# A two-layer gated-attention kernel: one more pair of projections by block products, and another order at the head of the output projection

## The chip, the cores and the metric

The kernel runs on one core of a Trainium2 chip. The metric is the time of one execution on the device in microseconds (us). A kernel is timed in several runs and the median is given. One further execution is profiled; its trace gives when each instruction started, how long it took and what ended the idle time before it. Five engines have a queue each and work their queue strictly in order: the tensor engine (PE, with its weight loads as PEld), the vector engine (DVE), the scalar engine (ACT), GpSimd (POOL) and the sync engine (SP), which only issues DMA transfers here.

## The reference, cut to what matters

One batch of 256 tokens with 2048 features goes through two layers, first gated linear attention (GLA), then retention, each with a gate path and an output projection, and a last RMS norm. Everything is float32. The change lies in the GLA layer:

```python
proj = rms_norm(h) @ w_in                     # 2048 -> q 1024, k 1024, v 4096, gate 4096
log_a = log_sigmoid((h @ w_a1) @ w_a2 + b_a) / 16
# four heads; per chunk of 64 tokens, with cum = cumsum(log_a):
scores = einsum('bhtk,bhsk,bhtsk->bhts', q, k, exp(cum_t - cum_s))    # causal
o      = scores @ v  + (q * exp(cum)) @ state
state  = exp(last) * state + (k * exp(last - cum)).T @ v
o      = o * rsqrt(mean(o * o) + eps) * head_g
out    = h + (o * silu(gate)) @ w_out         # 4096 -> 2048
```

## The kernel before, in words

**Tiles.** The 256 tokens are two halves of 128 partitions. A weight group is 2048 rows by 512 columns, cut into eight sub-blocks of 256 rows (512 KB each). A sub-block is loaded into one of eight `raw` buffers, and split into a rounded part `hi` (ACT, line 298) and a rest `lo` (DVE, line 299). There are four `hi` and four `lo` buffers, so a split can start only when the tensor engine is done with the sub-block four places earlier. Each product of float32 precision is three matmuls: left high by `hi`, left high by `lo`, left low by `hi`. A plain group is 8 sub-blocks x 2 row blocks x 2 token halves x 3 = 96 matmuls of 128x512.

**GLA heads.** `gla_head(h)` runs for four heads. It projects q and k (`gqk`), then for two groups of 512 columns the values (`gv`) and the gates (`gg`). Beside these, tasks in a queue called `side` are taken forward one step after each sub-block: the decay (`gla_decay`) and the scores (`gla_scores`). The scores work through seven levels (`w0` to `w6`) and a last product `w_x`: DVE makes exponents, ACT their exponential, DVE the products with q and k, PE a small matmul into `lv`. DVE then masks (`m`) what lies in `lv`, the seven levels are added into `s` on POOL (line 830, 14 instructions for a head), ACT and DVE split the sum into the pair `sc`, and `o_part` multiplies `sc` with a group's values (`go`, 9 matmuls). `og_part` norms and gates the result, and PE transposes (`got_tp`) bring it into `ogt`, the left side of the output projection.

**Pairs by block products.** Groups 5 and 7 (the second groups of heads 2 and 3) take values and gates together in `values_and_gates`: seven products of a half-size block scheme (`P1`, `P2`, `P3`, `P5` to `P8`, two sub-blocks of 6 matmuls each) and eight plain sub-blocks (`v4` to `v7`, `g4` to `g7`, 12 matmuls each) do the work of two plain groups. The string `UNIT` gives their order. The scheme needs sums of blocks of the left side (`xsum`, made by `make_sums` in the `rs` buffer) and of the weights: some are made by DMA that adds into a `raw` buffer (POOL's queue), some by DVE. Such a pair uses four PSUM banks A, B, C and V1, and a plain group two. The output projection of the first two heads (`ga`) is made of two such pairs in `out_pair`, whose left sums (`osum`) come from `ogt`. The residual x lies in `rs` from the start.

**What sets the order.** A scheduler puts each engine's instructions in an order that is fixed when the program is built; on the chip each engine takes its own in that order. An instruction marked `keep` is put behind whatever its engine was given before it in the code. The gate's SiLU in `g_evac` (line 688) is marked so, and the code of the last step of the scores, the copy into `sc` on ACT (line 724), stands right ahead of it for head 1. Weight splits are emitted three sub-blocks ahead of their use (`LOOK`).

Of the kernel before, what the change touches and what calls it, by code (L numbers as in the profile page):

```python
# [15 lines left out]
ALU = mybir.AluOpType  # L16

P = 128
# [46 lines left out]
def _plan():  # L65


    loads, subs = [], []

    def load(gid, j):  # L70
        loads.append((gid, j))
        return len(loads) - 1

    def use(c, pre=None, post=()):
        subs.append((c, pre, post))

    def plain(gid, js=range(NSUB)):
        for j in js:
            use(load(gid, j))

    def pair(g, v, q=None, order=None):
        order = (order or UNIT).split()
        x = [load(g, 0), load(g, 1)] if order[0] == "P1" else []
        z = []
        later = max(("P3", "P6"), key=order.index)
        for n, tok in enumerate(order):
            kind, i = tok[0], tok[1:]
            if kind in "qvg":
                plain({"q": q, "v": v, "g": g}[kind], [int(i)])
            elif tok == "z":  # L90
                z += [load(v, 2), load(v, 3)]
            elif tok == "P2":
                plain(g, [2, 3])
            else:
                if tok == "P1" and not x:
                    x += [load(g, 0), load(g, 1)]
                for j in range(2):
                    post = []
                    if tok == later:
                        post.append((z[j], (v, j)))  # L100
                    if tok == "P1":
                        post.append((x[j], (v, j)))
                    if tok == "P6":
                        post.append((x[j], (g, 2 + j)))
                    use(z[j] if tok in ("P3", "P7") else x[j], z[j] if tok == "P6" else None, post)

    def out_cols_of(name, half, cut, joint):
        for c in (0, 2):
            cols = [(name, half, c + n) for n in range(2)]
            if joint[c // 2]:  # L110
                pair(cols[1], cols[0])
                continue
            late = [range(NSUB)] if c or not cut else [range(cut), range(cut, NSUB)]
            for js in late:
                for x in cols:
                    plain(x, js)

    for half in range(2):
        for h in (2 * half, 2 * half + 1):
            plain(("aqk", h))  # L120
            for g in (2 * h, 2 * h + 1):
                if g in JOINT["a"]:
                    pair(("ag", g), ("av", g))
                else:
# [24 lines left out]
    buf = []  # L149
    for c in range(len(loads)):  # L150
        b = min([*range(NRAW), *_spare(loads[c])], key=lambda n: free[n])
        buf.append(b)
        free[b] = last[c]
    return loads, subs, places, last, buf


UNIT = "P1 v4 z P3 v5 P5 v6 P6 P2 v7 P7 g4 g5 P8 g6 g7"
MIXED = "q0 q1 P1 q2 q3 q4 z P5 q5 P6 q6 q7 P2 P3 v4 v5 v6 P7 v7 g4 g5 P8 g6 g7"
WHOLE = " ".join(f"q{j}" for j in range(NSUB)) + " " + UNIT


def ret_order(h):
# [4 lines left out]
HEAD = 4  # L167
EARLY = 2
JOINT = {
    "a": (5, 7),  # L170
    ("ao", 0): (True, True),
    ("ao", 1): (False, True),
    ("ro", 0): (False, True),
# [5 lines left out]
def kernel(  # L179
# [145 lines left out]
    def drain_side():  # L325
        while side:
            advance()
# [111 lines left out]
    def sums_in_v(name):  # L439
        return lambda n: v_p.tile([P, 2, QK, 2, P], F32R, tag="v", name=f"{name}{n}")  # L440

    def make_sums(lhs, name, where):
        s = cur["s"] = [None] * 4
        room = where(name)
        tt = nc.vector.tensor_tensor
        y = [t4_p.tile([P, QK, SEQ], F32, tag="t4", name=f"{name}_y{i}") for i in range(2)]
        for i in range(2):
            part = lhs[:, i * QK : (i + 1) * QK].bitcast(F32)
            tt(y[i], part[:, :, 0, :], part[:, :, 1, :], ALU.add)
# [4 lines left out]
        tt(f5, y[0][:, :, two], y[1][:, :, two], ALU.subtract)  # L454
        tt(f6, f5, y[0][:, :, one_], ALU.subtract)
        yield
        tt(f3, f6, y[1][:, :, one_], ALU.add)
        tt(f7, y[0][:, :, one_], y[0][:, :, two], ALU.subtract)
        yield
        for i, x in ((0, f3), (1, f5), (2, f6), (3, f7)):  # L460
            if i % 2 == 0:
                two_ = room(i // 2)
                s[i], s[i + 1] = two_[:, 0], two_[:, 1]
            keep(nc.scalar.activation(s[i][:, :, 0, :], x, AF.Copy))
            keep(tt(s[i][:, :, 1, :], x, s[i][:, :, 0, :].bitcast(F32), ALU.subtract))
            if i % 2:
                yield
# [285 lines left out]
    def gla_scores(h, box):  # L753
# [70 lines left out]
        nc.vector.tensor_scalar(s32[:, 1, :], ps[1][:, 3, :], SCALE, None, ALU.mult)  # L824
        yield
        for li, B in enumerate(LEVELS):
            for z in range(2):
                side_of = lambda a, h: a.rearrange("p (n h i) -> p n h i", h=2, i=B)[:, :, h, :]
                dst = side_of(s32[:, 2 * z, :], 1 - z)
                nc.gpsimd.tensor_tensor(dst, dst, side_of(m[:, li, :], z), ALU.add)  # L830
            if li == 3:
                yield
        yield
# [3 lines left out]
    def gla_head(h):  # L837
        hw = {}
        if h > 1:
            side.appendleft(gla_decay(h, hw))  # L840
        banks = None
        if h > 0:
            banks = acc(2, f"gqk{h}_ps", (P, 2, SEQ))
# [62 lines left out]
            )  # L906

        def joint_turn(tok):
            if tok == "v4":
                o_part(0)  # L910
            elif tok == "g5":
                o_part(1)
            else:
                advance()

        for gi in range(2):
            g = 2 * h + gi
            if g in JOINT["a"]:
                v = v_p.tile([P, 2, 2, GW], F32R, tag="v", name=f"gv{g}")
                sg = sg_p.tile([P, 2, GW], F32, tag="sg", name=f"gsg{g}")  # L920
                o = o_p.tile([P, 2, GW], F32, tag="o", name=f"ge{g}")
                vs.append(v)
                sgs.append(sg)
                banks = [slots[n] for n in (1, 0, 2, 3)]
                slots.rotate(-2)
                values_and_gates(
                    xhl, UNIT, acc(4, f"ge{g}_ps", which=banks), lambda: v, lambda: sg, lambda: o, r, r2, joint_turn
                )
                continue

            def v_hook(j):
                if h > 0 and gi == 1 and j == 1:
                    o_part(0)
                if h == 1 and gi == 1 and j > 1:
                    if j == 2:
                        cur["making"] = make_sums(ogt, "osum", sums_in_v)
                    if j < 6:
                        next(cur["making"])

            def g_hook(j):  # L940
# [4 lines left out]
                if gi == 1 and h == 1 and j == 3:  # L945
                    next(cur["making"])

            if h == 0 and gi == 1:
                drain_side()
# [36 lines left out]
    def out_pair(c, first, name, final=False):  # L986
# [36 lines left out]
        g = c + 1  # L1023
        cur["pin"] = final
        product(A, plain(0, 0), stop=True)
        advance()
        direct(lhs, (C, V1), 4)
        join(g, 0, A)
        advance()
        product(C, summed(0))  # L1030
        advance()
        direct(lhs, (C, V1), 5)
        drain_side()
        product(P5, summed(1), stop=True)
        direct(lhs, (C, V1), 6)
        for t in range(2):
            join(c, t, P5)
        product(A, summed(2), stop=True)
        product(B, plain(4, 0))
# [414 lines left out]

    for h in range(2):
        gla_head(h)
    slots = deque((2, 3, 0, 1))
    out_half(True, False, "ga", joint=JOINT["ao", 0])
    slots = deque((2, 3, 0, 1))
# [129 lines left out]
```

## Time and profile before

| what | value |
|---|---|
| time, median of 3 runs | 1372.14 us (1371.32 to 1372.71) |
| the profiled execution | 1371.82 us, span 1370.1 us |
| PE busy | 1360.1 us, 6564 matmuls |
| DVE, ACT, POOL busy | 1098.9, 846.7, 137.2 us |
| head 1: q and k / first group / second group | 126.98 to 152.24 / to 201.15 / to 248.90 us |
| output projection of the first two heads | 248.9 to 330.6 us |

The span leaves 1.7 us around it in the profiled execution. A busy time counts matmuls from issue to the modelled end, and they overlap; the time that one takes from the next is read from the distance of their starts in the timeline. A timeline row is start, length, engine, line, operation, output<-input, and in brackets the idle time ahead of it with what ended it.

### The profile page before, as it was taken

The page shows a single profiled execution, that of the slowest core. Times are in us where ns is not written, and L with a number is a line of the kernel's source. Part 1 is how long each engine was busy: PE and PEld are TensorE (multiplying, and loading weights), DVE is VectorE, ACT ScalarE, POOL GpSimd, SP SyncE. Part 2 cuts the span into 40 slices and gives each one's busy share as a digit, 9 for nine tenths or more (in the row PEclk, how much of TensorE's full clock was granted, in tenths as well). Part 3 has the DMA queues.
Part 4 walks back from the last instruction along what each step waited for, and adds up shares of the span by engine and source line. Part 5 has one row for each costly group of instructions (what it writes and reads, how often), then busy time and mean ns, then how long its engine had stood idle before and what let it go on. Part 6 is the DMA issues. An engine that isn't in the chain of part 4 may idle for free.

```text
span 1370.1 us, 18374 instructions
## 1 busy us (share of the span) xinstructions
PE 1360.1 (99%) x6564; PEld 1142.3 (83%) x6564; DVE 1098.9 (80%) x1520; ACT 846.7 (62%) x1119; POOL 137.2 (10%) x194
## 2 busy tenths in 40 slices
PE   9999999999999999999999999999999999999997
PEld 7888888888888888888888888888888888888886
DVE  6686795987878886769887988897867898889796
ACT  6576656656567756656666566655546666666565
POOL 1003020110021021001011010100101101010010
PEclk9999999999999999999999999999999999999999
DMA  9755565789658667868897878796798797879773
GB/s 363 255 175 168 169 208 184 154 251 316 202 154 259 201 207 180 326 169 232 260 336 199 259 203 249 209 320 212 172 365 219 245 253 208 268 188 322 237 177 124
DMA packets 84508, 315.04 MB, mean 230 GB/s; under 512 B 9776, under 2 KB 10800, under 8 KB 83136
## 3 DMA queue, kind: packets, MB, share of 16 engines
q1 hardware_dynamic: 67200, 241.63, 50.6%
q0 software_dynamic: 15920, 64.89, 23.7%
q10 hardware_dynamic: 1296, 7.35, 1.4%
q8 instruction: 51, 0.84, 0.2%
q14 instruction: 41, 0.34, 0.1%
HBM read 303.35 MB, written 10.49 MB: 229 GB/s over the span
## 4 chain that ended last, share of the span: by engine, by line
PE 99%; DMA 1%; DVE 0%; ACT 0%; issue 0%; DVEq 0%; ACTq 0%
PE rqk_ps L382 9%; PE re_ps L413 8%; PE re_ps L414 8%; PE re_ps L415 8%; PE rqk_ps L384 4%; PE gqk_ps L382 4%; PE gg_ps L342 3%; PE gv_ps L343 3%; PE gv_ps L341 3%; PE gv_ps L342 3%; PE gg_ps L343 3%; PE gg_ps L341 3%; PE gqk_ps L384 2%; PE ge_ps L415 2%; PE ge_ps L414 2%; PE ge_ps L413 2%
## 5 line engine op out<-in xcount | busy, mean ns | idle before, releaser
L299 DVE TENSOR_TENSOR lo<-raw,hi 128x1024 fp32r<-128x1024 f32 (+1 forms) x568 | 687.4, 1220 | 215.1 <-ACT hi L298 205.1
L298 ACT ACTIVATE hi<-raw 128x1024 fp32r<-128x1024 f32 (+1 forms) x568 | 596.3, 1056 | 398.9 <-PE rqk_ps L382 50.4
L382 PE MATMUL rqk_ps<-xhl,hi 128*128 128x512 f32 x512 | 160.0, 395 | 0.0
L415 PE MATMUL re_ps<-hi,xhl 128*128 128x512 f32 x352 | 137.1, 389 | 0.0
L414 PE MATMUL re_ps<-lo,xhl 128*128 128x512 f32 x352 | 137.1, 389 | 0.0
L413 PE MATMUL re_ps<-hi,xhl 128*128 128x512 f32 x352 | 132.3, 391 | 0.0
L310 POOL DMA_DIRECT2D raw<-in_w_all x90 | 78.0, 868 | 540.5 <-DVE lo L299 205.2
L384 PEld LDWEIGHTS rqk_ps<-xhl,lo 128*128 128x128 f32 x512 | 93.6, 188 | 20.3
L384 PE MATMUL rqk_ps<-xhl,lo 128*128 128x256 f32 x512 | 99.2, 279 | 0.0
L382 PEld LDWEIGHTS rqk_ps<-xhl,hi 128*128 128x128 f32 x512 | 80.7, 189 | 2.8
L382 PE MATMUL gqk_ps<-xhl,hi 128*128 128x512 f32 x256 | 79.5, 397 | 0.6 <-DVE xhl L550 0.6
L414 PEld LDWEIGHTS re_ps<-lo,xhl 128*128 128x128 f32 x352 | 66.1, 188 | 13.6
L415 PEld LDWEIGHTS re_ps<-hi,xhl 128*128 128x128 f32 x352 | 66.1, 188 | 13.6
L413 PEld LDWEIGHTS re_ps<-hi,xhl 128*128 128x128 f32 x352 | 65.9, 188 | 13.3
L342 PE MATMUL gg_ps<-lo,xhl 128*128 128x512 f32 x192 | 75.4, 393 | 0.0
L343 PE MATMUL gg_ps<-hi,xhl 128*128 128x512 f32 x192 | 75.1, 391 | 0.0
L342 PE MATMUL gv_ps<-lo,xhl 128*128 128x512 f32 x192 | 75.1, 391 | 0.0
L341 PE MATMUL gv_ps<-hi,xhl 128*128 128x512 f32 x192 | 75.0, 393 | 0.0
L341 PE MATMUL gg_ps<-hi,xhl 128*128 128x512 f32 x192 | 74.9, 391 | 0.0
L343 PE MATMUL gv_ps<-hi,xhl 128*128 128x512 f32 x192 | 74.8, 391 | 0.0
L830 POOL TENSOR_TENSOR s<-s,m 128x64 f32<-128x64 f32 x56 | 36.5, 684 | 232.3 <-DVE m L821 222.5
L384 PEld LDWEIGHTS gqk_ps<-xhl,lo 128*128 128x128 f32 x256 | 46.1, 188 | 10.0
(422 smaller groups left out, 2591.9 us busy)
## 6 DMA issues: line engine op xcount, KB each, us to landing
raw<-in_w_all SPq DMA_DIRECT2D x449, 512.0 KB, 4.9
raw<-in_w_all POOLq DMA_DIRECT2D x90, 512.0 KB, 7.2
resid<-in_x_n SPq DMA_DIRECT2D x2, 1024.0 KB, 9.8
gg<-in_gn_g POOLq DMA_DIRECT2D x8, 256.0 KB, 4.4
resid_x<-resid ACTq DMA_DIRECT2D x1, 2048.0 KB, 8.5
gb<-in_gn_b POOLq DMA_DIRECT2D x8, 256.0 KB, 4.9
gb_resid<-resid_x POOLq DMA_DIRECT2D x1, 2048.0 KB, 11.0
resid_g<-gb_resid ACTq DMA_DIRECT2D x1, 2048.0 KB, 9.0
```

Source lines behind the costliest of these rows:

```text
L298: a = nc.scalar.activation(hi[:, sl], src[:, sl], AF.Copy)
L299: b = nc.vector.tensor_tensor(lo[:, sl], src[:, sl], hi[:, sl].bitcast(F32), ALU.subtract)
L310: nc.gpsimd.dma_start(raws[n], block(key), accum_op=ALU.add)
L341: pin(mm(ps, xh, hi[:, q, :], start=kt == 0, stop=False, **onto))
L342: pin(mm(ps, xh, lo[:, q, :], start=False, stop=False, **onto))
L343: pin(mm(ps, xl, hi[:, q, :], start=False, stop=kt == end - 1, **onto))
L382: x = mm(ps[c], part, rhs[:, kt, :, :], start=kt == 0, stop=kt == NKT - 1)
L384: x = mm(ps[c][:, 0, :], part, rhs[:, kt, 0, :], start=False, stop=False)
L413: pin(mm(ps, xh, hi[:, q, :], start=start, stop=False, **again))
L414: pin(mm(ps, xh, lo[:, q, :], start=False, stop=False, **again))
L415: pin(mm(ps, xl, hi[:, q, :], start=False, stop=stop, **again))
L830: nc.gpsimd.tensor_tensor(dst, dst, side_of(m[:, li, :], z), ALU.add)
```

## The change

Group 3, the second group of head 1, is now taken as a pair as well. Its order is the string `FIRST`, with the product of scores and values of the first group after `v6` and that of the second after `g4`. The left sums `xsum1` for it are made in the `rs` buffer in head 1's q and k stage, over the residual, which is therefore loaded again from `x_n` after `P7`. The sums `osum` for the output projection are made in five steps during the pair. In the first pair of the output projection the three products that need only head 0's part of `ogt` (A, C, B) come first, with the string `HEADS` for its weights. The adding of the score levels goes from POOL, 14 instructions a head, to DVE, 7 a head, for all four heads.

```diff
+FIRST = "P1 v4 z P3 v5 P5 v6 P6 P2 v7 P7 P8 g4 g5 g6 g7"
+HEADS = "P1 z P3 P2 v4 v5 P5 v6 P6 v7 P7 g4 g5 P8 g6 g7"
 JOINT = {
-    "a": (5, 7),
+    "a": (3, 5, 7),
...
-                pair(cols[1], cols[0])
+                pair(cols[1], cols[0], order=HEADS if (name, half, c) == ("ao", 0, 0) else None)
...
-                    pair(("ag", g), ("av", g))
+                    pair(("ag", g), ("av", g), order=FIRST if g == 3 else None)
...
         for li, B in enumerate(LEVELS):
-            for z in range(2):
-                side_of = lambda a, h: a.rearrange("p (n h i) -> p n h i", h=2, i=B)[:, :, h, :]
-                dst = side_of(s32[:, 2 * z, :], 1 - z)
-                nc.gpsimd.tensor_tensor(dst, dst, side_of(m[:, li, :], z), ALU.add)
+            n = P // (2 * B)
+            dst = at(s32, B, (2 * P - B, 2), (2 * B, n), (1, B))
+            tt(dst, dst, at(m, li * P, (B, 2), (2 * B, n), (1, B)), ALU.add)
...
         if h > 1:
             side.appendleft(gla_decay(h, hw))
+        elif h == 1:
+            side.append(make_sums(xhl, "xsum1", sums_in_rs))
...
         def joint_turn(tok):
-            if tok == "v4":
+            if tok == ("v6" if h == 1 else "v4"):
                 o_part(0)
-            elif tok == "g5":
+            elif tok == ("g4" if h == 1 else "g5"):
                 o_part(1)
             else:
-                advance()
+                advance(2 if h == 1 and tok in ("g5", "g6", "g7") else 1)
+            if h == 1:
+                if tok == "P6":
+                    cur["making"] = make_sums(ogt, "osum", sums_in_v, "s_next")
+                if tok in ("P6", "P2", "v7", "P8", "g6"):
+                    next(cur["making"])
+                if tok == "P7":
+                    get_resid("resid_x")
...
-                if h == 1 and gi == 1 and j > 1:
-                    if j == 2:
-                        cur["making"] = make_sums(ogt, "osum", sums_in_v)
-                    if j < 6:
-                        next(cur["making"])
...
         product(A, plain(0, 0), stop=True)
-        advance()
-        direct(lhs, (C, V1), 4)
-        join(g, 0, A)
-        advance()
-        product(C, summed(0))
-        advance()
-        direct(lhs, (C, V1), 5)
-        drain_side()
-        product(P5, summed(1), stop=True)
...
+        if name == "ga" and c == 0:
+            advance()
+            product(C, summed(0))
+            advance()
+            product(B, plain(4, 0))
+            drain_side()
+            join(g, 0, A)
+            direct(lhs, (C, V1), 4)
+            direct(lhs, (C, V1), 5)
+            product(P5, summed(1), stop=True)
...
+        else:
...
     for h in range(2):
         gla_head(h)
+        cur["resid_at"] = x_n
+    cur["s"] = cur["s_next"]
```

Three places show what the change makes of the order. The first is the tensor engine at the end of head 1's first gate group; `lv` are the score levels, `go` is scores times values, `gg` and `gv` are the plain groups, `ge` is a pair's bank. Before, ahead of the first `go`:

```order
L343 MATMUL gv_ps_1947<-hi_1901,xhl 128x512
L341 MATMUL gv_ps_1946<-hi_1925,xhl 128x512
L342 MATMUL gv_ps_1946<-lo_1926,xhl 128x512
L698 MATMUL go_ps_1984<-gv_1741,sc_1850 128x512
L699 MATMUL go_ps_1984<-gv_1741,sc_1850 128x512
```

Now, at the same `go`:

```order
L417 MATMUL ge_ps_1956<-hi_1910,xhl 128x512
L766 MATMUL lv_1_1631<-w_4_1745 128x128 x2
L766 MATMUL lv_1_1631<-w_5_1778 128x128 x2
L766 MATMUL lv_1_1631<-w_6_1804 128x128 x2
L766 MATMUL lv_1_1631<-w_x 128x128 x2
L700 MATMUL go_ps_2082<-gv_1753,sc_1862 128x512
L701 MATMUL go_ps_2082<-gv_1753,sc_1862 128x512
L700 MATMUL go_ps_2083<-gv_1753,sc_1862 128x512
L701 MATMUL go_ps_2083<-gv_1753,sc_1862 128x512
L415 MATMUL ge_ps_1958<-hi_1930,xhl 128x512
```

Before, 42 matmuls of 128x512 stood between the last `lv` product and the first `go`; now none does, and `v4` (the last row, into bank C) stands behind the `go`.

The second is the vector engine from the last product of the scores' chain on; `osum` are the left sums of the output projection, `m` the masked levels, `s` their sum. Now:

```order
L817 TENSOR_TENSOR w_x<-w_x,qk_1527 128x256
L823 TENSOR_TENSOR m_1863<-lv_0_1630,mask 128x512
L301 TENSOR_TENSOR lo_1971<-raw_1842,hi_1970 128x1024
L451 TENSOR_TENSOR osum_y_2128<-ogt 128x1024
L301 TENSOR_TENSOR lo_1982<-raw_1865,hi_1981 128x1024
L451 TENSOR_TENSOR osum_y_2129<-ogt 128x1024
L825 TENSOR_TENSOR m_1863<-lv_1_1631,mask 128x384
L826 TENSOR_SCALAR s_1_1633<-lv_1_1631 128x128
L456 TENSOR_TENSOR osum_f_2156<-osum_y_2128,osum_y_2129 128x512
L831 TENSOR_TENSOR s_1_1633<-s_1_1633,m_1863 128x2x64
L831 TENSOR_TENSOR s_1_1633<-s_1_1633,m_1863 128x2x32x2
L831 TENSOR_TENSOR s_1_1633<-s_1_1633,m_1863 128x2x16x4
```

Four more of line 831 follow. Up to `osum_f` the order of the chain is the old one (there the split stood ahead of the first `m`), and the seven adds are new on this engine.

The third is the scalar engine behind the same chain; `gsg` is the SiLU of the gates. Now:

```order
L815 ACTIVATE w_x<-w_x 128x512
L300 ACTIVATE hi_1970<-raw_1842 128x1024
L300 ACTIVATE hi_1981<-raw_1865 128x1024
L726 ACTIVATE sc_1862<-s_1_1633 128x384
L690 ACT_TABLE_LOAD
L690 ACTIVATE gsg_1950<-gg_ps_1758,rr 128x512
L690 ACTIVATE gsg_1950<-gg_ps_1759,rr 128x512
```

The copy into `sc` is still followed by the table load and the two SiLU, but what stands in the two banks that they read is now awaited by `v4`, where before the next group had two other banks.

More of the change, by code (lines that the diff above doesn't have):

```diff
@@ L440, in sums_in_v, with make_sums @@
         return lambda n: v_p.tile([P, 2, QK, 2, P], F32R, tag="v", name=f"{name}{n}")
-    def make_sums(lhs, name, where):
-        s = cur["s"] = [None] * 4
+    def make_sums(lhs, name, where, key="s"):
+        s = cur[key] = [None] * 4
         room = where(name)
@@ L926, in gla_head @@
                 values_and_gates(
-                    xhl, UNIT, acc(4, f"ge{g}_ps", which=banks), lambda: v, lambda: sg, lambda: o, r, r2, joint_turn
+                    xhl, FIRST if h == 1 else UNIT, acc(4, f"ge{g}_ps", which=banks), lambda: v, lambda: sg, lambda: o, r, r2, joint_turn
                 )
@@ L944, in g_hook @@
                     o_part(1)
-                if gi == 1 and h == 1 and j == 3:
-                    next(cur["making"])
             if h == 0 and gi == 1:
@@ L1025, in out_pair @@
         product(A, plain(0, 0), stop=True)
-        advance()
-        direct(lhs, (C, V1), 4)
-        join(g, 0, A)
-        advance()
-        product(C, summed(0))
-        advance()
-        direct(lhs, (C, V1), 5)
-        drain_side()
-        product(P5, summed(1), stop=True)
[L1035 to L1039, printed above, removed]
+        if name == "ga" and c == 0:
[8 more added lines that the diff above has]
+            product(P5, summed(1), stop=True)
+            direct(lhs, (C, V1), 6)
+            for t in range(2):
+                join(c, t, P5)
+            product(A, summed(2), stop=True)
+        else:
+            advance()
+            direct(lhs, (C, V1), 4)
+            join(g, 0, A)
+            advance()
+            product(C, summed(0))
+            advance()
+            direct(lhs, (C, V1), 5)
+            drain_side()
+            product(P5, summed(1), stop=True)
+            direct(lhs, (C, V1), 6)
+            for t in range(2):
+                join(c, t, P5)
+            product(A, summed(2), stop=True)
+            product(B, plain(4, 0))
         join(c, 0, A, ALU.subtract)
```

## The prediction

> **What bounds the kernel now.** I read the page's busy line and chain of waits first, then the stages around the change.
>
> ```profile
> span 1370.1 us, 18374 instructions
> PE 1360.1 (99%) x6564; PEld 1142.3 (83%) x6564; DVE 1098.9 (80%) x1520; ACT 846.7 (62%) x1119; POOL 137.2 (10%) x194
> ...
> PE 99%; DMA 1%; DVE 0%; ACT 0%; issue 0%; DVEq 0%; ACTq 0%
> ```
>
> The chain that ended last is matmul work throughout: one matmul less is a gain, and any wait of the tensor engine is a loss that nothing later gives back. The stages of head 1 (q and k, first group, second group) and the first pair of the projection, in a table by stretches (PE, PEld, DVE, ACT, POOL busy, granted clock, DMA):
>
> ```profile
> 126.98:152.24 25.26, 25.26 (x146) 22.03 (x145) 16.44 (x31) 16.04 (x26) 0.00 (x0) 1.00 0.52 164
> 152.24:201.15 48.91, 48.91 (x239) 41.17 (x238) 41.44 (x73) 28.77 (x40) 7.03 (x11) 1.00 0.63 199
> 201.15:248.90 47.75, 47.75 (x214) 39.51 (x212) 29.59 (x42) 28.77 (x39) 3.79 (x7) 1.00 0.60 168
> 248.90:290.00 41.10, 41.10 (x192) 34.11 (x190) 36.22 (x40) 27.08 (x33) 5.17 (x6) 1.00 0.85 242
> ```
>
> PE is busy in all of it. DVE has 85% and 88% in the second and last, so it is the engine that can make PE wait if it gets more to do there. The timeline of PE at the first product of scores and values:
>
> ```profile
> 196.36 0.60 PE L764 MATMUL lv<-w 128*128 128x128 f32 x4
> 196.72 0.48 PE L342 MATMUL gg_ps<-lo,xhl 128*128 128x512 f32 x1
> 197.04 0.60 PE L764 MATMUL lv<-w_x 128*128 128x128 f32 x4
> ...
> 201.15 0.39 PE L341 MATMUL gv_ps<-hi,xhl 128*128 128x512 f32 x1
> ...
> 207.04 0.39 PE L698 MATMUL go_ps<-gv,sc 128*128 128x512 f32 x1
> ```
>
> From 201.15 to 207.04 stand 26 matmuls of 128x512, so each takes 5.89 / 26 = 0.2265 us, not the 0.39 of its row. A small one takes 0.36 / 4 = 0.09. Between the last score product (197.04) and the first `go` (207.04) PE has 10 us of other work.
>
> **What is removed.** A plain pair of groups is 192 matmuls, seven products and eight sub-blocks are 7 x 12 + 8 x 12 = 180. Twelve less: 12 x 0.2265 = 2.7 us. No other matmul is added or dropped.
>
> **The wait for the scores.** In the new order PE has nothing between the last `lv` product and `go`, so PE waits out the chain on DVE and ACT. That chain runs before as well, hidden behind PE's 10 us; its rows on DVE, POOL and ACT:
>
> ```profile
> 188.14 0.28 DVE L798 TENSOR_TENSOR w<-ref,lc 128x128 f32<-128x128 f32 x1
> 188.35 0.29 DVE L799 TENSOR_TENSOR w<-lc 128x128 f32<-128x128 f32 x1
> ...
> 190.22 1.22 DVE L299 TENSOR_TENSOR lo<-raw,hi 128x1024 fp32r<-128x1024 f32 x1
> 191.36 0.42 DVE L802 TENSOR_TENSOR w<-w,qk 128x256 f32<-128x256 f32 x1
> 191.70 0.42 DVE L803 TENSOR_TENSOR w<-w,qk 128x256 f32<-128x256 f32 x1
> ...
> 192.37 0.42 DVE L815 TENSOR_TENSOR w_x<-w_x,qk 128x256 f32<-128x256 f32 x1
> ...
> 195.41 1.32 DVE L449 TENSOR_TENSOR osum_y<-ogt 128x1024 f32<-128x1024 f32 x1 [0.88 <-PE lv L764]
> 196.65 1.37 DVE L299 TENSOR_TENSOR lo<-raw,hi 128x1024 fp32r<-128x1024 f32 x1
> 197.94 1.34 DVE L449 TENSOR_TENSOR osum_y<-ogt 128x1024 f32<-128x1024 f32 x1
> 199.21 0.54 DVE L823 TENSOR_TENSOR m<-lv,mask 128x384 f32<-128x384 f32 x1
> 199.67 0.28 DVE L824 TENSOR_SCALAR s<-lv 128x128 f32<-128x128 f32 x1
> 199.87 0.70 DVE L454 TENSOR_TENSOR osum_f<-osum_y,osum_y 128x512 f32<-128x512 f32 x1
> ```
> ```profile
> 194.68 8.45 POOL L830 TENSOR_TENSOR s<-s,m 128x64 f32<-128x64 f32 x14 [32.34 <-DVE m L821]
> ```
> ```profile
> 201.35 1.06 ACT L298 ACTIVATE hi<-raw 128x1024 fp32r<-128x1024 f32 x1 [1.63 <-PE gg_ps L343]
> 203.17 0.53 ACT L724 ACTIVATE sc<-s 128x384 fp32r<-128x384 f32 x1 [0.75 <-POOL s L830]
> 203.71 1.28 ACT L688 ACT_TABLE_LOAD   x1
> 205.00 1.27 ACT L688 ACTIVATE gsg<-gg_ps,rr 128x512 f32<-128x512 f32 x2
> ```
>
> By distances of starts, from the end of the product `w_x`: the first `m`, 512 elements, 0.6 (as `osum_f`, of the same size); split 1.14 (190.22 to 191.36); `osum_y` 1.24; split 1.14; `osum_y` 1.27; second `m` 0.46; `s` 0.20; `osum_f` 0.6. That is 6.7 us. Seven adds of 128 elements, each waiting for the one before: 0.21 us if they overlap like line 798, 0.33 if a whole row of 0.29 and a start must pass; I take 0.29, 2.0 us. The copy into `sc`, 0.53, and 0.1 for signals. In all 9.3 us, in which PE does the pair of `lv` matmuls, 0.2. **First term: 9.1 us.** Its floor is 8.2 (adds at 0.21 and no signals), its ceiling 10.6: from `w_x`'s end at 192.8 to the end of `sc` at 203.7 the old chain took 10.9, with POOL and an idle 0.88 and 0.75 in it.
>
> Ahead of it, `w_x` itself is late. In the new order the `w4` work can start only when the `lv` matmuls of `w0` have run, in the middle of the last gate sub-block, for its buffer is theirs; and the split of `v4`, ahead of it on DVE, ends some 0.9 us later still (a buffer free 6 matmuls earlier, then 1.06 on ACT, 1.14 on DVE). Then DVE has 13 rows of 128x256 at 0.34 (191.36 to 191.70), one `w_x` pair among them, two of 0.2 and a split: 0.9 + 4.8 + 0.4 + 1.1 = 7.2. PE has 8 small matmuls, 6 and 12 large ones: 0.7 + 4.1 = 4.8, and 0.5 of `lv` while it waits. **Second term: 1.9 us**, floor 0 (before, `w_x` was ready at 192.8, 4.3 us ahead of PE), ceiling 3 (the `lv` products not overlapped, and a signal each).
>
> Behind it, `v4` needs bank C, which the SiLU of the gates still reads, and the SiLU is queued behind the copy into `sc` and a table load: 1.29 (203.71 to 205.00) and 0.64, less four `go` matmuls of 0.9. **Third term: 1.0 us**, floor 0.8, ceiling 1.7. The Trainium skill, page "ScalarE: Activation LUTs", section "What ACT_TABLE_LOAD costs", puts a switch of sets at 1.28 us for the load and 1.38 for a drain, 2.66 in all. The row here has 1.28 and the next starts 0.01 after it, so this trace shows no drain; by the page the third term would be an estimated 2.4 and the total 1.4 higher.
>
> **The clock after the wait.** PE never idles so long here; the nearest row is the program's start:
>
> ```profile
> 1.00 4.03 PE L522 MATMUL warm_ps<-warm 128*128 128x128 f32 x20 [1.00 <-POOL lnone L524]
> ```
>
> Twenty small matmuls take 4.0 us, 0.20 each, against 0.09 in the middle. If an idle 9 us brings that back, PE loses about half of 4 us, 2.0, of which 0.9 falls on the `go` matmuls and so into the SiLU's wait. **Fourth term: 0.8 us**, floor 0, ceiling 2. The Trainium skill, "TensorE: Matmul & The Clock Gate", Part 1, says the same in mechanism: half rate after an idle window of about 3.4 us, full rate after about 3.4 us of work. By it the term would be an estimated 1.7 less the covered part.
>
> **The head of the projection.** The first pair now opens with six sub-blocks of 6 matmuls, 1.36 us each, and DVE's order up to the transposes of group 3 holds, besides their splits, head 1's norm and gating. DVE's groups of that stretch before, busy and mean:
>
> ```profile
> L299 DVE TENSOR_TENSOR lo<-raw,hi 128x1024 fp32r<-128x1024 f32 x23 | 28.2, 1228 | 14.8 <-ACT hi L298 14.8
> L896 DVE SCALAR_TENSOR_TENSOR go<-go,hr,gsg 128x512 f32<-128x512 f32 x4 | 2.9, 750 | 0.5 <-ACT gsg L688 0.4
> L502 DVE SCALAR_TENSOR_TENSOR ogt<-got_tp,smalls,ogt 128x256 fp32r<-128x256 f32 x6 | 2.8, 476 | 0.0
> ...
> L293 DVE TENSOR_TENSOR raw<-raw,raw 128x1024 f32<-128x1024 f32 x2 | 2.4, 1216 | 0.0
> ...
> L497 DVE TENSOR_TENSOR hr_nw<-hr_nw 128x2 f32<-128x2 f32 x3 | 0.5, 159 | 0.1
> ```
>
> Eight splits at 1.14 = 9.1, four gatings at 0.7 = 2.8, three `ogt` at 0.4 = 1.2, two weight sums 2.3, 13 small ones at 0.2 = 2.6, the gate's sum 0.6: 18.6 us. PE has 58 large and 8 small matmuls there, 13.9. DVE starts some 0.7 early, so PE is short by 4.0 if DVE does not get further ahead. **Fifth term: 3.0 us**, nearer to 4 than to none; floor 0 (before, 88% of DVE left no wait here), ceiling 5.
>
> **What is hidden.** `xsum1` on DVE in the q and k stage: two rows of 1.33, four of 0.7, four splits of 0.69, 8.2 us, into a stage in which DVE is free for 25.26 - 16.44 = 8.8; if that fails, PE waits up to 2. Six more splits and two weight sums (9.1 us of DVE, 6.4 of ACT) lie in the pair, where DVE was 62% busy; the stall gives them time. The adds of heads 2 and 3 cost DVE 2 us a head and free POOL. Six more adding transfers join POOL's queue, and the residual comes again:
>
> ```profile
> raw<-in_w_all POOLq DMA_DIRECT2D x90, 512.0 KB, 7.2
> ...
> gb_resid<-resid_x POOLq DMA_DIRECT2D x1, 2048.0 KB, 11.0
> ```
>
> It is issued after `P7`; 60 matmuls of the pair and more than 58 of the projection, 26 us, pass before the first join needs it, against 11. Without that cover the joins, and the splits behind them on DVE, would be up to 11 late.
>
> **Sum.** -2.7 + 9.1 + 1.9 + 1.0 + 0.8 + 3.0 = +13.1. The profiled execution took 1371.8 (1370.1 of span, 1.7 around it), so 1384.9; the median is 0.3 above it: 1385.2. I forecast **1385 us**, slower by 0.9%, with a chance of 0.68. All floors give -2.7 + 8.2 + 0 + 0.8 = +6.3, 1378.5; all ceilings -2.7 + 10.6 + 3 + 1.7 + 2 + 5 = +19.6, 1391.7.
>
> **Rivals.**
> 1. *Only the scores' wait.* The projection's head is covered and the clock holds: -2.7 + 9.1 + 1.9 + 1.0 = +9.3, 1381.4. For it: this scheduler's orders left PE no wait before. Against: DVE's 18.6 us. Chance 0.18.
> 2. *The other side: the scores come in time.* DVE's adds replace 8.45 us of POOL, `sc` is ready before the product P1 ends, and PE waits nowhere: 1372.1 - 2.7 = 1369.4, faster. It decides from the point where the last add ends before PE's last `lv` matmul plus 0.6. For it: before, DVE was 4.3 us ahead at `w_x`. Against: `m` reads what that very matmul writes, so at least 0.46 + 0.2 + 7 x 0.21 + 0.53 = 2.7 of chain always follow, and the split and `osum` rows stand in between. Chance 0.08, half of it below 1369.4.
> 3. *A second late transfer.* The residual's 2 MB or an adding transfer comes late on POOL's queue: up to 11 more, about 1392 to 1396. Against: 26 us of cover. Chance 0.06.
>
> **Chances and range.** What a measurement of this kernel can tell from no change is about 0.2%, 2.7 us. Faster 0.04 (half of rival 2), same 0.04, slower 0.92. The range from 1378.5 to 1391.5 holds the forecast and rival 1 with their unknown costs and leaves out rivals 2 and 3.
>
> **What would show it.** A PE row of `go` with an idle of about 9 us, released by ACT's copy into `sc` (term one); idle of about 2 us ahead of the `lv` products (two) and 1 us ahead of the first `v4` matmul (three); matmuls of 128x512 at 0.4 instead of 0.23 behind it (four); idle up to 2 us ahead of the `got_tp` transposes or the products in the projection's head (five); 6552 matmuls, and the rest as before. If `go` starts within 1 us of the last `lv` product, the prediction is wrong at its root.

## The result, and the profile after

The changed kernel takes 1387.5 us (median of 5 runs, 1386.34 to 1388.13) against 1372.14: 1.0109 times the time before, 95% interval 1.0097 to 1.0122. Forecast were 1385 us and 1378.5 to 1391.5. Its profiled execution has a span of 1385.7 us, 15.6 more than before. The page's busy line and its chain of waits:

```profile
span 1385.7 us, 18370 instructions
PE 1362.5 (98%) x6552; PEld 1142.0 (82%) x6552; DVE 1121.0 (81%) x1571; ACT 855.5 (62%) x1133; POOL 106.3 (8%) x145
...
PE 92%; DVE 3%; DMA 3%; ACT 1%; issue 1%; POOL 0%; DVEq 0%; ACTq 0%; POOLq 0%
```

The chain was 99% PE; now other engines hold 7% of it. The view of PE's waits (line, engine waited for; us in all, times, longest) names the places:

```profile
PE go_ps L700 <- ACT sc L726: 8.4, 1, 8.4
PE got_tp L710 <- DVE ogt L504: 1.6, 1, 1.6
PE gae_ps L416 <- DVE lo L301: 1.2, 2, 0.8
...
PE gae_p L416 <- DVE lo L301: 0.9, 1, 0.9
PE go_ps L700 <- ACT gv L1412: 0.6, 1, 0.6
```

The timeline of PE shows the long wait and what follows it:

```profile
203.87 0.71 PE L766 MATMUL lv<-w_x 128*128 128x128 f32 x4
212.99 0.80 PE L700 MATMUL go_ps<-gv,sc 128*128 128x512 f32 x1 [8.41 <-ACT sc L726]
213.59 0.63 PE L701 MATMUL go_ps<-gv,sc 128*128 128x512 f32 x1
...
214.99 0.80 PE L415 MATMUL ge_ps<-hi,xhl 128*128 128x512 f32 x1
215.59 0.63 PE L416 MATMUL ge_ps<-lo,xhl 128*128 128x512 f32 x1
216.01 0.63 PE L417 MATMUL ge_ps<-hi,xhl 128*128 128x512 f32 x1
```

From 213.59 on the starts lie 0.43 us apart, not 0.2265. The table by stretches has the reason in its clock column (the third number from the end), 0.50 from 206.71 to 216.95:

```profile
206.71:216.95 10.24, 3.96 (x9) 2.74 (x10) 7.83 (x16) 3.56 (x5) 0.00 (x0) 0.50 0.17 54
216.95:220.36 3.41, 3.41 (x17) 2.80 (x16) 0.27 (x1) 1.06 (x1) 0.00 (x0) 1.00 0.00 0
```

The chain on DVE and ACT during the wait:

```profile
203.72 0.70 DVE L823 TENSOR_TENSOR m<-lv,mask 128x512 f32<-128x512 f32 x1
204.32 1.23 DVE L301 TENSOR_TENSOR lo<-raw,hi 128x1024 fp32r<-128x1024 f32 x1
205.45 1.23 DVE L451 TENSOR_TENSOR osum_y<-ogt 128x1024 f32<-128x1024 f32 x1
...
209.52 0.70 DVE L456 TENSOR_TENSOR osum_f<-osum_y,osum_y 128x512 f32<-128x512 f32 x1
210.12 2.26 DVE L831 TENSOR_TENSOR s<-s,m 128x128 f32<-128x128 f32 x7
```
```profile
212.41 0.52 ACT L726 ACTIVATE sc<-s 128x384 fp32r<-128x384 f32 x1 [9.02 <-DVE s L831]
212.96 1.28 ACT L690 ACT_TABLE_LOAD   x1
214.25 1.26 ACT L690 ACTIVATE gsg<-gg_ps,rr 128x512 f32<-128x512 f32 x2
```

These are the forecast's rows, each without a gap; the first SiLU ends at about 214.9 and `v4` starts at 214.99.

Where the 15.6 us lie: the projection's first matmul starts at 258.95 instead of 248.89 (+10.1), the first matmul of head 2's q and k at 346.09 instead of 330.58 (+15.5), and from there to the end nothing is added. In matmul starts beyond their usual distance: 8.6 at `go`, 0.9 in the `lv` products, 2.1 in the 9 matmuls from it on (0.13 of this is the wait of `v4`, the rest the half speed), 1.6 at the second `go` (at 241 us), 3.8 at 268 to 277 us, 1.1 at 289 us and 0.45 more than before at the end of the second pair: 18.5, less 2.7 for the twelve matmuls, 15.8.

### The profile page after: what moved, and what is told of

The parts are those of the page before. It is cut to its first block, busy times and chain, and to the rows that moved or that the text cites. A ratio compares the mean times of both kernels' runs of the same rounds, so it can differ in the third digit from the quotient of the medians.

```text
span 1385.7 us, 18370 instructions
## 1 busy us (share of the span) xinstructions
PE 1362.5 (98%) x6552; PEld 1142.0 (82%) x6552; DVE 1121.0 (81%) x1571; ACT 855.5 (62%) x1133; POOL 106.3 (8%) x145
## 4 chain that ended last, share of the span: by engine, by line
PE 92%; DVE 3%; DMA 3%; ACT 1%; issue 1%; POOL 0%; DVEq 0%; ACTq 0%; POOLq 0%
PE rqk_ps L384 9%; PE re_ps L415 8%; PE re_ps L416 8%; PE re_ps L417 8%; PE rqk_ps L386 4%; PE gqk_ps L384 4%; PE gv_ps L345 3%; PE gv_ps L343 3%; PE gv_ps L344 3%; PE gg_ps L344 3%; PE gg_ps L345 3%; PE gg_ps L343 3%; PE ge_ps L415 3%; PE ge_ps L416 2%; PE ge_ps L417 2%; PE gqk_ps L386 2%
## 5 line engine op out<-in xcount | busy, mean ns | idle before, releaser
L301 DVE TENSOR_TENSOR lo<-raw,hi 128x1024 fp32r<-128x1024 f32 (+1 forms) x574 | 694.4, 1220 | 218.5 <-ACT hi L300 206.7
L312 POOL DMA_DIRECT2D raw<-in_w_all x96 | 83.0, 866 | 656.1 <-DVE lo L301 415.2
L344 PE MATMUL gv_ps<-lo,xhl 128*128 128x512 f32 x160 | 62.9, 393 | 0.0
L344 PE MATMUL gg_ps<-lo,xhl 128*128 128x512 f32 x160 | 62.8, 393 | 0.0
L345 PE MATMUL gv_ps<-hi,xhl 128*128 128x512 f32 x160 | 62.5, 392 | 0.0
L345 PE MATMUL gg_ps<-hi,xhl 128*128 128x512 f32 x160 | 62.5, 390 | 0.0
L343 PE MATMUL gg_ps<-hi,xhl 128*128 128x512 f32 x160 | 62.4, 392 | 0.0
L343 PE MATMUL gv_ps<-hi,xhl 128*128 128x512 f32 x160 | 62.4, 394 | 0.0
L416 PE MATMUL ge_ps<-lo,xhl 128*128 128x512 f32 x132 | 51.7, 392 | 0.0
## 6 DMA issues: line engine op xcount, KB each, us to landing
resid<-in_x_n SPq DMA_DIRECT2D x2, 1024.0 KB, 11.9
gb_resid<-resid_x POOLq DMA_DIRECT2D x1, 2048.0 KB, 11.9
```

Of the source, the lines that this page charges most:

```text
L301: b = nc.vector.tensor_tensor(lo[:, sl], src[:, sl], hi[:, sl].bitcast(F32), ALU.subtract)
L312: nc.gpsimd.dma_start(raws[n], block(key), accum_op=ALU.add)
L343: pin(mm(ps, xh, hi[:, q, :], start=kt == 0, stop=False, **onto))
L344: pin(mm(ps, xh, lo[:, q, :], start=False, stop=False, **onto))
L345: pin(mm(ps, xl, hi[:, q, :], start=False, stop=kt == end - 1, **onto))
L416: pin(mm(ps, xh, lo[:, q, :], start=False, stop=False, **again))
```

## The experiments

Ratios are to the kernel before, run beside each.

**The adds alone (e4).** Of the kernel before, only this is changed (14 instructions a head on GpSimd, 7 on DVE):

```
...
-                nc.gpsimd.tensor_tensor(dst, dst, side_of(m[:, li, :], z), ALU.add)
...
+            tt(dst, dst, at(m, li * P, (B, 2), (2 * B, n), (1, B)), ALU.add)
```

> The edit: the kernel before, with only the adding of the score levels moved from GpSimd (14 instructions a head) to the vector engine (7 a head), all else as before. If the adds cost nothing by themselves (the tensor engine has 10 us of other work between the last lv product and go in that order): 1372.1 us within 1 us. If the vector engine's 2 us a head reach the tensor engine: up to 4 x 2 = 8 us more, about 1374 to 1380.

1372.15 us, ratio 1.0003 (0.9994 to 1.0013). The adds cost nothing where PE has other work.

**What holds PE at the long wait? First, `go` out of the way (e2).** `pin` is `keep` for head 1's first group:

```
-                mm(ps[t], ah, v[:, s, 0, :], start=n == 0, stop=False)
+                pin(mm(ps[t], ah, v[:, s, 0, :], start=n == 0, stop=False))
```

> The edit: the changed kernel, but the four products of scores and values of the first group are pinned behind v6 in the tensor engine's order, so go no longer stands ahead of v4. Theory A (bank C): v4 still starts only when the first SiLU is done, at about 214.9 us of the span as now; go's 9 matmuls are then work that is no longer done under that wait, 1 us later: 1387.5 to 1389 us, an idle of about 10 us ahead of the first v4 matmul, released by the scalar engine's SiLU. Theory B (go waits for the scores): the tensor engine goes on with v4 to v6 and the wait is hidden: about 1378 us.

1393.07 us, 1.0155 (1.0137 to 1.0173). PE's waits, and the stretch of low clock:

```profile
PE ge_ps L415 <- ACT gsg L690: 10.4, 1, 10.4
PE go_ps L700 <- ACT gv L1412: 2.3, 1, 2.3
```
```profile
207.25:220.90 13.65, 6.15 (x15) 4.81 (x16) 7.05 (x16) 4.13 (x6) 0.00 (x0) 0.50 0.10 38
```

With `go` gone from the place, PE still idles, now 10.4 us and for the SiLU. So it is not the product of scores and values alone that waits for the scores: `v4`, and with it all that stands behind it in PE's queue, does so too, since `v4` needs a bank of the gates, the SiLU frees it, and the SiLU is queued behind the copy into `sc`. It came out dearer than either theory said: in the profiled execution 15 matmuls ran at half speed, and the second `go` waited 2.3 us. That execution was the longest of four (1390.37 to 1395.61), so the two sizes may be at their upper end.

**Then the SiLU out of the queue (e1).**

```
         yield
+        if h == 1:
+            yield
         split_scores(s32.rearrange("p b n -> p (b n)"), sc)
```

> The edit: the changed kernel, but the copy of head 1's scores into sc is written one step later, so that the two SiLU of the first group's gates are no longer pinned behind it on the scalar engine. Theory A (the queue of the scalar engine holds bank C: the tensor engine has no work because v4 needs the bank that the SiLU reads): the idle 8.4 us ahead of go and the half-clock matmuls behind it (about 2 us over their full-clock time) go, and nothing of like size takes their place: 1387.5 - 8.6 - 2.0 = about 1377 us. Theory B (the scores' chain on the vector engine is too long for whatever stands in front of go): v4 and P3 cover at most 24 x 0.227 = 5.4 us of the wait, so 3 us and the slow clock remain: about 1382 us.

1394.85 us, 1.0167 (1.0152 to 1.0183), slower than the change itself, and neither forecast. The long wait is gone, as theory A had it, but other waits stand elsewhere (first row: in all, times, longest):

```profile
PE ge_ps L415 <- ACT hi L300: 6.1, 3, 4.7
PE got_tp L710 <- DVE go L901: 5.3, 2, 4.4
```

Back from the 4.7 us at 233 us: the split `hi` waits for a transfer (first row), the transfers bunch, and POOL's adding transfers had stood 22.8 us for a weight sum on DVE, which DVE reached only at 217 us:

```profile
232.43 1.06 ACT L300 ACTIVATE hi<-raw 128x1024 fp32r<-128x1024 f32 x1 [2.59 <-DMA raw<-in_w_all]
```
```profile
199.00:225.00 26.00, 22.35 (x100) 16.93 (x99) 20.88 (x31) 18.93 (x22) 3.40 (x4) 1.00 0.48 135
225.00:258.00 33.00, 28.06 (x115) 22.38 (x114) 24.34 (x31) 20.38 (x28) 2.33 (x4) 0.90 0.98 313
```
```profile
218.87 0.87 POOL L312 DMA_DIRECT2D raw<-in_w_all  x1 [22.84 <-DVE raw L295]
```

The DMA share (last number but one) goes from 0.48 to 0.98. DVE had hardly a gap from 208 to 231 us. That the long wait had given DVE time which the new order needs (theory D in what follows) is the reading; this run alone doesn't show it, for the edit did more than move the copy. The two SiLU now stand among the exponentials of the last score levels, so ACT loads its tables four times there, 1.28 us each (at 198.43, 200.44, 202.38 and 205.33 us), where the change has one load (212.96), and DVE stood 1.98 and 2.19 us for ACT before 206 us.

**The sums off DVE (e5).** The four sums `osum_f` likewise:

```
+        su = nc.gpsimd.tensor_tensor if key == "s_next" else tt
-            tt(y[i], part[:, :, 0, :], part[:, :, 1, :], ALU.add)
+            su(y[i], part[:, :, 0, :], part[:, :, 1, :], ALU.add)
```

> The edit: the changed kernel, but the sums osum of the output projection's left side (two of 128x1024, four of 128x512) are added on GpSimd instead of the vector engine; nothing else. Theory C (the rows of the vector engine that stand between the last lv product and sc set the length of the first wait): two rows of 1.14 us and one of 0.6 leave the chain, so the idle ahead of go falls from 8.4 to about 5.5 us and the time to about 1384.5 us; less still if the later waits shrink with it. Rival: the sums come too late from the slower GpSimd for the third product of the reordered head, and that wait takes the gain: 1387 to 1390 us.

1389.43 us, 1.0129 (1.0114 to 1.0144), and the wait at `go` grew to 9.6 us. The two splits in the chain and GpSimd's rows beside them:

```profile
204.34 6.05 DVE L301 TENSOR_TENSOR lo<-raw,hi 128x1024 fp32r<-128x1024 f32 x2
```
```profile
203.12 6.18 POOL L452 TENSOR_TENSOR osum_y<-ogt 128x1024 f32<-128x1024 f32 x2 [6.85 <-PE lv L767]
```

Two splits take 2.35 us elsewhere; beside a GpSimd sum they took 6.05. So this run did not shorten the chain and doesn't test theory C.

**The sums later on DVE (e9).** For the `osum` of the first pair alone:

```
-            tt(y[i], part[:, :, 0, :], part[:, :, 1, :], ALU.add)
+            (keep if key == "s_next" else lambda x: x)(tt(y[i], part[:, :, 0, :], part[:, :, 1, :], ALU.add))
```

> The edit: the changed kernel, but the two first sums osum_y of the output projection's left side are pinned on the vector engine where the code has them (behind the splits of P6's time), so that no row of osum stands between the last lv product and sc any more; they stay on the vector engine, GpSimd has nothing to do beside it. Theory C (the vector engine's rows between the last lv product and sc set the length of the first wait; the longer wait of the fifth experiment came from GpSimd slowing the vector engine's rows): the idle ahead of go falls by 1.14 + 1.14 + 0.6 = 2.9 us to 5.5, and the time to 1384.5 us. If C is wrong, the idle stays at 8.4 us or above, and the time at 1387 us or more.

```profile
PE go_ps L700 <- ACT sc L726: 5.7, 1, 5.7
PE got_tp L710 <- DVE go L899: 5.3, 2, 4.6
```
```profile
204.56 2.35 DVE L301 TENSOR_TENSOR lo<-raw,hi 128x1024 fp32r<-128x1024 f32 x2
```

The wait fell by 2.7 us, as theory C said: DVE's rows set its length. The time did not: 1393.21 us, 1.0149 (1.0132 to 1.0166). The projection starts 2.5 us earlier than in the change (256.44 against 258.95) but takes 7.5 us longer (to 351.04 against 346.09): the transposes in its head wait 5.3 us for the gating, for which they had not waited at all. Two things differ on DVE there. The sums now stand in its way at 234 to 253 us. And the steps of head 1's norm, which the gating needs, are placed differently: in the change three splits stand between them, and from the first step to the gating they take 5.9 us (258.81 to 264.76); here seven splits and two weight sums stand between them, and they take 11.9 us (261.97 to 273.88). How much of the loss comes from the sums and how much from that order is not shown.

**The idle filled (e8, e11).** Matmuls whose results nobody reads, behind the last `lv` product; 45 on top of e2 (e11), 90 on the changed kernel (e8):

```
         pair_mm(ps[1][:, 3, :], w)
+        if h == 1:
+            idle = mis_p.tile([P, P], F32, tag="mis", name="idle")
+            for _ in range(45):
+                mm(idle, w[:, 1, 0:P], w[:, 1, SEQ : SEQ + P], start=True, stop=True)
```

> The edit: the changed kernel with 90 matmuls of 128x128 into an unused bank put between head 1's last lv product and what follows (their results are not read; they take about 9 us of the 10 us for which v4 must wait). Clock theory (the half-speed matmuls behind the first wait come from the idle itself): the first v4 matmuls run at 0.227 us instead of 0.43 and the granted clock stays at 1.00 there; v4 still starts when the SiLU has freed its bank, at about 215 us, and go's 9 matmuls come later: against the second experiment (1393.1 us, go also behind v4, 14 matmuls at half speed) about 3 us less. If the slow matmuls had another cause (the weights' transfers, the bank), they stay at 0.43 us and the time at about 1393 us.

> The edit: the kernel of the second experiment (go pinned behind v6, 1393.1 us, idle of 10.4 us ahead of v4 and 14 matmuls of 0.43 us behind it) with 45 matmuls (90 instructions of about 0.11 us, 10 us; twice that many in the eighth were 20 us and outlasted the wait) into an unused bank right behind the last lv product. Clock theory: the idle is gone or under 1 us, v4 starts at about 215 us as before, its matmuls take 0.227 us and the granted clock stays 1.00: 2.8 us less than the second experiment, about 1390.3 us. Otherwise about 1393 us.

In e8 the 90 became 180 instructions of 20 us, which outlasted the wait: 1397.28 us, 1.0188 (1.0173 to 1.0204), no measure of the time, though the clock stayed at 1.00. e11, on top of e2:

```profile
204.32 10.21 PE L824 MATMUL idle<-w_x 128*128 128x128 f32 x90
214.41 0.50 PE L415 MATMUL ge_ps<-hi,xhl 128*128 128x512 f32 x1
214.75 0.39 PE L416 MATMUL ge_ps<-lo,xhl 128*128 128x512 f32 x1
214.98 0.40 PE L417 MATMUL ge_ps<-hi,xhl 128*128 128x512 f32 x1
```

1388.97 us, 1.0124 (1.0109 to 1.0139), 4.1 less than e2 with 90 instructions more; e2's runs lie so far apart that the size is rough. `v4` starts about where it did (214.41 against 214.75), and at full speed: the starts lie 0.23 us apart, not 0.43. The second `go` then waited no 2.3 us either. Idle costs twice: while it lasts, and in the slow matmuls behind it.

**The old head of the projection (e3).** With the old branch of `out_pair` to match:

```
-                pair(cols[1], cols[0], order=HEADS if (name, half, c) == ("ao", 0, 0) else None)
+                pair(cols[1], cols[0], order=None)
```

> The edit: the changed kernel with the old order of the first pair of the output projection (A, v4, C, v5, P5 and so on; table of weights to match). If the reordered head (six sub-blocks of 6 matmuls at the start against a vector engine with 18.6 us of work) is what makes the waits of 3.8 us at 268 to 277 us and of 1.1 us at 289 us, they go: about 1383 us, and with the first wait untouched 1386 at the least change. If it is the vector engine's work alone (norm, gating, sums of the left side, which come in either order), the waits stay or move to other rows: 1386.5 to 1388.5 us.

1389.16 us, 1.0129 (1.0112 to 1.0146), above both forecasts.

```profile
PE gae_ps L417 <- DVE ogt L504: 1.6, 1, 1.6
PE gae_ps L415 <- ACT gsg L1422: 1.2, 1, 1.2
PE got_tp L710 <- DVE go L899: 1.1, 2, 0.9
```

The waits of the head stay, in other rows: `HEADS` is not their cause. In either order DVE's and ACT's rows end them; that DVE's amount of work is the cause is argued from this, not shown.

**Scores earlier (e7, e10) and the DVE relieved (e6).** In e7 head 1's decay starts in its q and k stage, with `osum` on GpSimd; e10 has the decay and e9's later sums; e6 is e1 with `osum` on GpSimd.

```
-        if h > 1:
+        if h > 0:
             side.appendleft(gla_decay(h, hw))
...
```

> The edit: the kernel of the first experiment (SiLU ahead of the copy into sc, 1394.9 us) with the sums osum on GpSimd as well. Theory D (without the first wait the vector engine is busy from 208 to 231 us without a gap, frees the raw buffers late, and so the transfers and the tensor engine come late): some 4 us of vector work leave that stretch, the wait of 4.9 us at 233 us shrinks by about as much, 1389 to 1391 us. Rival E (the transfers themselves are the bound, 98% busy from 225 to 258 us there): no change beyond 1 us, 1394 to 1396 us.

> The edit: the changed kernel with head 1's decay started three steps earlier (in its q and k stage, as in heads 2 and 3), so that the scores' steps and sc are written three sub-blocks ahead of the SiLU; and the sums osum on GpSimd. If the first wait is all that the new order lacks: 1387.5 less 8.6, 2.0 and some of the later waits, 1374 to 1377 us, and go no longer waits. If the vector engine's total work in this part is the deeper bound (as theory D has it), the wait comes back elsewhere, as in the first experiment: 1383 to 1392 us.

> The edit: the decay of head 1 three steps earlier (as in the seventh experiment) and osum_y later (as in the ninth); nothing on GpSimd. In the seventh experiment the rows of the vector engine beside GpSimd took 2.3 to 3.0 us instead of 1.22, about 7 us in all, and the tensor engine waited 4.7 us for late transfers at 234 us. If it was this slowing that made the buffers and transfers late, the wait at 234 us goes, no first wait comes back, and the waits of the projection's head (4.4 us) remain: 1375 to 1379 us. If the vector engine's total work is too much even at full speed, as theory D says: 1380 to 1386 us.

e6: 1390.39 us, 1.0133 (1.0116 to 1.015), in theory D's range, and 4.5 less than e1. The wait for transfers, 4.7 us in e1, is 0.4 here, so the transfers were not a bound by themselves (rival E); but with GpSimd slowing DVE and new waits the run tells little more. e7: 1386.41 us, 1.0103 (1.0088 to 1.0118): `go` no longer stalls, and 4.5 us of late transfers come in its place. e10: 1381.73 us, 1.0072 (1.0057 to 1.0087), the best version, yet in theory D's range:

```profile
PE got_tp L710 <- DVE go L899: 5.2, 2, 4.6
PE gae_p L416 <- DVE lo L301: 1.4, 1, 1.4
...
PE gae_ps L416 <- DVE lo L301: 0.8, 1, 0.8
```

Group 3 takes 48.0 us there (199.29 to 247.26), with little waiting, and the projection starts 1.6 us earlier than in the kernel before (248.89). All of the loss lies in the projection, which takes 92.3 us (to 339.59) against 81.7. DVE's order in its head has the norm's small steps between splits:

```profile
251.96 0.15 DVE L891 TENSOR_TENSOR hm<-sso 128x2 f32<-128x2 f32 x1
...
257.13 0.15 DVE L499 TENSOR_TENSOR hr_nw<-hr_nw 128x2 f32<-128x2 f32 x1
257.20 1.22 DVE L301 TENSOR_TENSOR lo<-raw,hi 128x1024 fp32r<-128x1024 f32 x1
...
263.87 2.74 DVE L899 SCALAR_TENSOR_TENSOR go<-go,hr,gsg 128x512 f32<-128x512 f32 x4
```

The same steps in the change, with three splits between them where e10 has nine rows of 1.14 us:

```profile
258.81 0.15 DVE L891 TENSOR_TENSOR hm<-sso 128x2 f32<-128x2 f32 x1
...
264.76 2.74 DVE L899 SCALAR_TENSOR_TENSOR go<-go,hr,gsg 128x512 f32<-128x512 f32 x4
```

So e10 doesn't show that DVE has too much work in all (theory D): the order of this chain is a rival. With the change's order the gating would come 6.0 us earlier (11.9 less 5.9, an estimate from these rows), more than the 5.2 us of wait; what the rows put off by it would then hold up is not known, and e10 with that order was not run.

**The norm's steps on GpSimd (e12).** On top of e10, for head 1's `rsqrt`:

```
...
+            g = nc.gpsimd
+            for it in range(3):
+                g.tensor_tensor(a, b, b, ALU.mult)
+                g.tensor_tensor(a, a, m, ALU.mult)
+                g.tensor_scalar(a, a, -0.5, 1.5, ALU.mult, ALU.add)
+                g.tensor_tensor(y if it == 2 else b, a, b, ALU.mult)
...
```

> The edit: the kernel of the tenth experiment (decay earlier, osum_y later, 1381.7 us), with the nine small steps of head 1's rsqrt (128x2 each) taken from the vector engine, where each stands behind a split of 1.14 us (251.96 to 263.87 us for the whole norm), to GpSimd as twelve steps; nothing else. Theory F (the head's wait is this chain's latency, stretched by the splits between its steps): the gating comes 3 us or more earlier, the wait of 4.8 us ahead of the transposes shrinks by as much, and if less than 2 us of it is left the slow matmuls behind it (2.4 us in all) go as well: 1375.5 to 1378.5 us. Rival: the vector engine's splits alone keep the tensor engine back there, and the wait only moves to them: 1380.5 to 1382.5 us.

```profile
PE got_tp L718 <- DVE go L907: 3.4, 2, 2.5
...
PE gae_ps L417 <- DVE ogt L512: 1.1, 1, 1.1
```

1382.52 us, 1.0077 (1.006 to 1.0094): no gain, at the upper end of the rival's range. The gating came 2.2 us earlier (262.13 against 263.87, in a run that was 0.4 later by then) and the wait in front of it shrank, but 1.1 us returned at `ogt`, behind a weight sum and two splits. The run isn't a clean one: DVE stood 2.3 us for GpSimd's steps, which are slow beside its splits (the last section). How much of the head's wait is DVE's amount of work, and how much the order in which it stands, stays open: this run took the steps off DVE but left the splits and the first weight sum ahead of the gating. No version beat the kernel before.

## Why the prediction was right, point by point

- **Twelve matmuls, 2.7 us**: 6552 matmuls, as counted.
- **First term (wait for the scores), 9.1**: 8.6 measured. Its split, sums, masks and adds stand in the profile as listed. Its account was half of the cause: it said that PE has nothing between `lv` and `go`; e2 shows that without `go` PE would wait longer, for the SiLU's bank. The third term had named that queue, but as an effect behind `go`.
- **Second term (`w_x` late), 1.9**: 0.9. DVE's rows behind the split of `v4` were counted as 4.8 + 0.4 + 1.1 = 6.3 us and took 6.6 (197.16 to 203.72), with 15 rows of 128x256. What was too low is PE's side: beside the 18 large matmuls 24 small ones of `lv` stood there before the wait (16 from 196.04 on, `w0`'s among them, and 8 from 201.92 on), where I counted 8.
- **Third term (SiLU's bank), 1.0**: 0.13. The four `go` matmuls at half speed took 1.9 us instead of the 0.9 that I subtracted, and covered almost all of it. The drain that the Trainium skill adds to a table load ("ScalarE: Activation LUTs", "What ACT_TABLE_LOAD costs") does not show: the first SiLU starts 1.29 us after the load does (212.96 to 214.25).
- **Fourth term (clock), 0.8**: 2.0. I halved the 4 us of the program's start and took off what `go` covers. The low clock lasted 3.96 us of work, about as long as there, and each of its 9 matmuls cost 0.2 more. The 0.9 that I took off is booked here and not in the third term; the two together were 1.8, measured 2.1.
- **Fifth term (the projection's head), 3.0**: 3.8 at 268 to 277 us, 1.1 at 289 us. The size was low. Of its two causes `HEADS` was wrong: e3 keeps the waits without it. That DVE is short there (18.6 us of work) fits, since DVE has no gap from 261.21 us to the end of these waits at 276.77, but no run shows it apart from the order of DVE's rows.
- **Missed**: 1.6 at the second `go`, for which `FIRST` puts the product right behind `P8` while the values' split is still to come (`go_ps` waits for `gv`).
- **Slips in the working**: thirteen rows of 0.34 make 4.4 us and not 4.8 (second term), 2.0 less 0.9 is 1.1 and not 0.8 (fourth), and the first term's floor is 8.4 by its own rule, not 8.2. They move the sum by 0.1.
- **What is hidden**: right. No wait of PE in the q and k stage, none for the residual, and from head 2 on 1039.6 us against 1039.5.

The rivals "in time" and "a second late transfer" fell; the "only the scores' wait" rival had 1381.4, and lacked the head's waits. The long wait and the clock came as forecast. That the sum held as well as it did, 15.8 us of losses forecast against 18.5, is in part luck: the first three terms were too high by 2.4 us in all, and this took off half of what the other two and the missed waits were short by.

## What to carry to other kernels

A queue worked in order passes a wait on: ask of each engine not only what waits, but what is pinned behind it and what that holds (here a copy holds a SiLU, the SiLU a bank, the bank the next product). When one engine is at 99%, a saving of its work must be paid by engines with room at that very place; taking a wait away elsewhere may only move it, as in e1 and e9. There the order of other engines changed too, so compare their rows before blaming their amount of work. Price idle of the tensor engine with the slow matmuls behind it.

## What the runs showed of the hardware

**The clock.** In this case's traces the clock is 0.50 for 10.24 us (the change), 13.65 and 3.41 (e2) or 6.83 (e10, from 262.73 us on), all multiples of 3.41. After the long idle it comes back only after 3.96 us (the change) or 6.15 us (e2) of work. The Trainium skill, "TensorE: Matmul & The Clock Gate", Part 1, tells of a free-running window of 3413 ns, which agrees with the grid; it speaks of about 3.4 us of work for the way back, and here it was up to 6.15. It asks an idle window of about 3.4 us for the drop; an idle of 2.34 us was enough in e2, and the low clock began 1.4 us after the work had resumed:

```profile
246.80 0.73 PE L700 MATMUL go_ps<-gv,sc 128*128 128x512 f32 x2 [2.34 <-ACT gv L1412]
```
```profile
248.21:251.62 3.41, 3.41 (x9) 2.65 (x9) 3.32 (x4) 0.92 (x1) 0.00 (x0) 0.50 0.97 413
```

**GpSimd and VectorE hinder each other, both ways.** A split of 1.23 us took 3.0 beside a GpSimd sum (e5). A GpSimd step of 128x2 took 1.09 us beside DVE's splits and 0.19 alone (e12):

```profile
255.39 1.09 POOL L500 TENSOR_TENSOR hr_nw<-hr_nw 128x2 f32<-128x2 f32 x1 [10.13 <-DVE hr_nw L496]
...
259.97 0.19 POOL L500 TENSOR_TENSOR hr_nw<-hr_nw 128x2 f32<-128x2 f32 x1
```

The Trainium skill, "Trainium Architecture — The Big Picture", section "What this means for kernel authors", says that the two share a port under an exclusive lock. The rows agree, and give its price here: the third and fourth of GpSimd's steps in e12 ended at 258.75 and 259.89 us, each 0.05 us after a row of DVE (258.70 and 259.84), as if they had had to wait that row out.
